# Two-layer attention trunk on one core: q/k copies by DMA, P normalised on ScalarE, and half of the gate projections moved beside branch A's heads

## Chip, core and metric

One core of a Trainium2 chip runs the whole program in one launch. The metric is device time in microseconds (us), from the first to the last instruction of the core. The kernel before was timed three times: 1426.5 us is the median (1426.38 to 1427.1).

## What is computed

A decoder trunk of two layers on 512 tokens of width 1024, all in float32. The reference, cut to one layer:

```python
hdn = rms_norm(x, norm_w)
qa, ka, va, za, qb, kb, vb, zb, ga, gb = split_cols(hdn @ w_in)      # ten blocks of 1024 columns
ya = dilated_mixture(rope(qa), rope(ka), va) * silu(za)              # branch A: 16 heads of 64
ob = diff_attention(rope(qb), rope(kb), vb, lam)                     # branch B: softmax(1) - lam * softmax(2)
yb = rms_norm(ob, subln_w) * (1 - lam_init) * silu(zb)               # 8 heads of 128
merged = sigmoid(ga) * (ya @ w_proj_a) + sigmoid(gb) * (yb @ w_proj_b)
x = x + merged @ w_out
```

After the second layer comes a last RMS norm.

## The kernel before

Every float32 operand of a product is split in two float32r parts, high and low, and each product is three matmuls: high by high, high by low, low by high (lines 282 to 284). A weight block of 128x1024 is loaded by SyncE (line 96), its high part is made on ScalarE (`whi`, line 102) and its low part on VectorE (`wlo`, line 103). A projection (`proj_T`) is a chunk of two such blocks: 48 matmuls of 512 columns, which give two PSUM tiles `pj` (b = 0 and b = 1). Three such PSUM tiles exist; an eviction function turns each into what it is for.

The work of a layer stands in this order: two z chunks and the two v products; then part a, with branch A's heads 0 to 7; part b, with branch B's heads 0 to 6; part c, with B's last head; then the four `pb` chunks and the four output chunks. In parts a to c a main list of chunks is given by the table `parts()`, and the attention steps of the heads are spread evenly among the chunks (`merge`). A scheduler then orders each engine's instructions, and each engine works in that order.

The steps of this study touch the following places. A `qk` chunk gives q (b = 0) and k (b = 1) for a unit: two heads of A, or one of B. Its eviction `ev_qk` (line 398) shuffles the tile on VectorE (`sw`, line 401), multiplies by the rotary tables (line 403 on VectorE, line 404 on GpSimd) and adds (line 405). Then it writes, in 64-partition pieces, the high and low parts of q to `qx` and of k to two tiles `kx`: six ScalarE and six VectorE instructions for a unit (lines 410 to 413, and 419 to 422 twice). The scores need high and low stacked on partitions, so the halves are crossed over.

The attention step of A for one half (one head) makes four blocks of scores (lines 480 to 487), exponentials (line 488, ScalarE, which also sums the denominators), and then `norm` multiplies the four blocks of P by the reciprocal denominators on VectorE (line 531). P is transposed by TensorE (line 506), evicted as high and low (`pt`, lines 507 and 508) and multiplied by v (`o`, line 538). B's `comb` scales both P's (lines 579 to 583).

A `gate` chunk evicts both gates of one row block m (line 693), takes the sigmoid (line 695), and on GpSimd multiplies the A gate by A's projection, which `pa` had written to DRAM and which is loaded back (lines 677 to 697). `pb` adds B's part (lines 704 and 705). In part a stand eight qk and three z chunks, in part b seven qk, the four pa, three z and gates 0 and 1, in part c gates 2 to 7.

Of the kernel before, what the change touches and what calls it, by code (L numbers as in the profile page):

```python
# [23 lines left out]
BIG = 1e30  # L24
SWAP = [(i ^ 8) if i < 16 else i for i in range(32)]
# [7 lines left out]
def trunk_kernel(ctx: ExitStack, tc: tile.TileContext, x, ws, norm_w, subln_w, final_w, lams, negb, rope, ident_in,  # L33
# [15 lines left out]
    x1_dram = dram.tile([DEPTH - 1, NB, P, T], F32, name="x1_dram")  # L49
    v_dram = dram.tile([DEPTH, 2, 8, P, 4, P], F32, name="v_dram")  # L50
# [217 lines left out]
    def proj_T(what, rhs, evac, first=False):  # L268
# [5 lines left out]
        def step(b, k):  # L274
            if b == 0 and k == 0:
                prep_to(j0 + 2)
            if k == 0:
                pool, tag = (pss, "s") if first else (psj, "pj")
                hold[b] = pool.tile([P, T], F32, tag=tag, name=f"pj{c}_{b}")
            ps, hb, o = hold[b], rhs(k), 256 * (k % 4) + b * P  # L280
            w_h, w_l = whi[j0 + k // 4][:, o:o + P], wlo[j0 + k // 4][:, o:o + P]
            nc.tensor.matmul(ps, w_h, hb[:, 0], start=(k == 0), stop=False)  # L282
            nc.tensor.matmul(ps, w_h, hb[:, 1], start=False, stop=False)  # L283
            nc.tensor.matmul(ps, w_l, hb[:, 0], start=False, stop=(k == 7))  # L284
            if b == 1 and k == 3:
                prep_to(j0 + 3)
            if k == 7 and first and b == 1:
                rstd_cols()
                layer_tables()
                for bb in range(2):  # L290
                    evac(bb, hold.pop(bb))
            if k == 7 and not first:
                evac(b, hold.pop(b))
# [103 lines left out]

    def ev_qk(key):
        def f(b, ps):
# [6 lines left out]
            lo, hi = slice(0, 64), slice(64, 128)  # L406
# [114 lines left out]
    def a_pair(layer, u):  # L521
# [48 lines left out]
    def b_head(layer, u):  # L570
# [4 lines left out]
        def comb():  # L575
            r = [small.tile([P, 4], F32, tag=f"rb{h}", name=f"rb{key}{h}") for h in range(2)]
            for h in range(2):
                nc.vector.reciprocal(r[h], store["den", h])
            nc.vector.tensor_scalar(r[1], r[1], nlam[:, layer:layer + 1], None, OP.mult)
            for i in range(4):  # L580
                p, p2 = store["p", 0][i], store["p", 1][i]
                nc.vector.tensor_scalar(p, p, r[0][:, i:i + 1], None, OP.mult)
                nc.vector.scalar_tensor_tensor(p, p2, r[1][:, i:i + 1], p, OP.mult, OP.add)

        def pv(half):
# [16 lines left out]
            for n in range(2):  # L602
                i = 2 * half + n
                scr = small.tile([P, P], F32, tag="sqs", name=f"sqs{key}{i}", bufs=2)
                nc.scalar.activation(scr, o[:, n], AF.Square, accum_out=store["ss"][:, i:i + 1])
            if half == 1:
                r = store["ss"]
                inv_sqrt(r, r, 1.0 / P, 1e-5)
                for i in range(4):
                    nc.vector.tensor_scalar(store["o"][:, i], store["o"][:, i], r[:, i:i + 1], None, OP.mult)  # L610
# [88 lines left out]
    def pb(layer, i):

# [9 lines left out]
        return lambda: proj_T((layer, "pb", i), lambda k: st_["y"][layer, 1, k], ev)  # L710
# [283 lines left out]
```

## Time and profile before

| what | us |
|---|---|
| median of three timed runs | 1426.5 |
| the profiled execution's own time | 1429.07 |
| its span, first to last instruction | 1427.3 |
| TensorE busy | 1376.5 (96%) |
| VectorE busy | 1102.9 (77%) |
| ScalarE busy | 879.0 (62%) |
| GpSimd busy | 166.5 (12%) |

The profile was taken on one execution. A matmul's row begins when it starts, and its end is modelled; since matmuls are pipelined, a row of TensorE overlaps the next one, and a gap between two starts can be partly covered by the row before it. Branch A's heads lie at about 130 to 380 us in the first layer and 830 to 1080 us in the second; branch B's follow, up to about 620 and 1320 us.

### The profile page before, as it was taken

To read this page: it belongs to the slowest core of one execution; us is meant where nothing else is said; L and a number is where in the kernel's file an instruction comes from. 1 tells how busy PE (TensorE), PEld (TensorE's weight loads), DVE (VectorE), ACT (ScalarE), POOL (GpSimd) and SP (SyncE) were. 2 spreads that over 40 slices of the span, in tenths; PEclk is the share of its full clock that TensorE was granted. 3 is DMA by queue.
4 is the path that set the end of the run, shared out by engine and by line. 5 is a ranking of instruction groups with operands and counts; after the bars stand their busy time and mean duration, and the time that the engine had idled before them with its cause. 6 is when DMAs were issued, how large, how long until landed. Compare 5 with 4: busy or idle time off the path is not lost.

```text
span 1427.3 us, 19038 instructions
## 1 busy us (share of the span) xinstructions
PE 1376.5 (96%) x6728; PEld 1144.1 (80%) x6728; DVE 1102.9 (77%) x2252; ACT 879.0 (62%) x1630; POOL 166.5 (12%) x139
## 2 busy tenths in 40 slices
PE   7999999999999999999999999999999999999998
PEld 5788777878788888888878887777878888888898
DVE  6876999999967898645466879999998688975554
ACT  8665667667665668632566666667766567774333
POOL 4100110110101120110220011010110011111000
PEclk9999999999999999999999999999999999999999
DMA  9643222212233323333585242212223322243421
GB/s 300 166 118 118 78 86 65 75 54 82 70 118 101 95 91 110 110 108 103 182 266 132 60 133 82 63 64 82 68 73 96 123 92 85 86 125 94 165 90 66
DMA packets 64607, 152.57 MB, mean 107 GB/s; under 512 B 6016, under 2 KB 22528, under 8 KB 64512
## 3 DMA queue, kind: packets, MB, share of 16 engines
q1 hardware_dynamic: 45312, 134.57, 29.4%
q0 software_dynamic: 2304, 8.39, 3.3%
q10 hardware_dynamic: 16896, 8.39, 2.0%
q8 instruction: 53, 0.87, 0.2%
q14 instruction: 42, 0.34, 0.1%
HBM read 134.55 MB, written 16.78 MB: 106 GB/s over the span
## 4 chain that ended last, share of the span: by engine, by line
PE 67%; DVE 19%; issue 7%; ACT 5%; DMA 1%; POOL 1%; SPq 0%; POOLq 0%; DVEq 0%; ACTq 0%
PE pj L282 16%; PE pj L283 16%; PE pj L284 16%; DVE wlo L103 3%; DVE pt L508 2%; PE X L303 1%; PE X L304 1%; PE X L302 1%; PE pv L302 1%; PE pv L304 1%; PE pv L303 1%; ACT whi L102 1%; DMA T<-ws_d 1%; PE Y L303 1%; POOL sq L206 1%
## 5 line engine op out<-in xcount | busy, mean ns | idle before, releaser
L282 PE MATMUL pj<-h,whi 128*128 128x512 f32 x1024 | 410.1, 402 | 15.0 <-DVE whi L801 6.5
L283 PE MATMUL pj<-h,whi 128*128 128x512 f32 x1024 | 408.0, 398 | 1.2 <-DVE h L189 1.1
L284 PE MATMUL pj<-h,wlo 128*128 128x512 f32 x1024 | 405.6, 398 | 0.0
L102 ACT ACTIVATE whi<-raw 128x1024 fp32r<-128x1024 f32 x207 | 218.7, 1057 | 173.2 <-PE pj L283 114.2
L103 DVE TENSOR_TENSOR wlo<-raw,whi 128x1024 fp32r<-128x1024 f32 x207 | 258.5, 1249 | 83.0 <-ACT whi L102 82.7
L282 PEld LDWEIGHTS pj<-h,whi 128*128 128x128 f32 x1024 | 195.5, 191 | 59.5 <-issue 6.4
L284 PEld LDWEIGHTS pj<-h,wlo 128*128 128x128 f32 x1024 | 195.3, 191 | 39.2 <-DVE wlo L103 0.3
L283 PEld LDWEIGHTS pj<-h,whi 128*128 128x128 f32 x1024 | 195.3, 191 | 39.1 <-DVE h L189 2.9
L103 DVE TENSOR_TENSOR wlo<-T,whi 128x1024 fp32r<-128x1024 f32 x24 | 31.2, 1300 | 14.9 <-ACT whi L102 14.8
L696 POOL TENSOR_TENSOR g<-g,pr 128x512 f32<-128x512 f32 x16 | 21.2, 1326 | 148.0 <-ACT g L695 148.0
L303 PE MATMUL pv<-wlo,mg 128*128 128x256 f32 x128 | 35.7, 283 | 0.0
L304 PE MATMUL pv<-whi,mg 128*128 128x256 f32 x128 | 35.7, 283 | 0.0
L302 PE MATMUL pv<-whi,mg 128*128 128x256 f32 x128 | 35.4, 283 | 0.0
L704 DVE TENSOR_TENSOR g<-pj,g 128x512 f32<-128x512 f32 x16 | 11.1, 692 | 30.5 <-PE pj L284 30.5
L102 ACT ACTIVATE whi<-T 128x1024 fp32r<-128x1024 f32 x24 | 25.1, 1055 | 8.6 <-PE pj L283 2.9
L206 POOL TENSOR_TENSOR sq<-sq,sq 128x512 f32<-128x512 f32 x12 | 19.7, 1638 | 88.6 <-issue 53.4
L708 ACT ACTIVATE mg<-g 128x512 fp32r<-128x512 f32 x16 | 10.1, 632 | 29.5 <-DVE g L705 29.5
L488 ACT ACT_TABLE_LOAD x21 | 26.9, 1283 | 0.3
L302 PE MATMUL X<-whi,h 128*128 128x512 f32 x64 | 24.1, 402 | 2.5 <-DVE z(0, 0, 0)_292 L453 2.5
L693 DVE TENSOR_TENSOR g<-pj,rb 128x512 f32<-128x512 f32 x32 | 22.0, 686 | 5.7 <-PE pj L284 5.6
L303 PE MATMUL X<-wlo,S 128*128 128x512 f32 x64 | 25.1, 393 | 0.8 <-DVE wlo L103 0.8
L303 PE MATMUL Y<-wlo,S 128*128 128x512 f32 x64 | 25.0, 391 | 0.8 <-DVE wlo L103 0.8
(4176 smaller groups left out, 3279.9 us busy)
## 6 DMA issues: line engine op xcount, KB each, us to landing
raw<-ws_d SPq DMA_DIRECT2D x199, 512.0 KB, 3.7
T<-ws_d POOLq DMA_DIRECT2D x16, 512.0 KB, 7.5
v_dram<-c ACTq DMA_DIRECT2D x24, 256.0 KB, 2.6
pa_dram<-pa SPq DMA_DIRECT2D x16, 256.0 KB, 3.1
pr<-pa_dram SPq DMA_DIRECT2D x16, 256.0 KB, 4.0
v_dram<-v ACTq DMA_DIRECT2D x8, 256.0 KB, 5.9
xr<-x_d SPq DMA_DIRECT2D x8, 256.0 KB, 4.4
x_dram<-xr SPq DMA_DIRECT2D x8, 256.0 KB, 3.2
```

The costliest lines, as they stand in the source:

```text
L102: nc.scalar.activation(whi[j], src, AF.Copy)
L103: nc.vector.tensor_tensor(wlo[j], src, bits(whi[j]), OP.subtract)
L206: nc.gpsimd.tensor_tensor(st_["acc"], st_["acc"], s, OP.add)
L282: nc.tensor.matmul(ps, w_h, hb[:, 0], start=(k == 0), stop=False)
L283: nc.tensor.matmul(ps, w_h, hb[:, 1], start=False, stop=False)
L284: nc.tensor.matmul(ps, w_l, hb[:, 0], start=False, stop=(k == 7))
L302: nc.tensor.matmul(ps, hh, w_h, start=first, stop=False, skip_group_check=True)
L303: nc.tensor.matmul(ps, hh, w_l, start=False, stop=False, skip_group_check=True)
L304: nc.tensor.matmul(ps, hl, w_h, start=False, stop=last, skip_group_check=True)
L488: nc.scalar.activation(p, p, AF.Exp, bias=mn[:, i:i + 1], scale=-1.0, accum_out=den[:, i:i + 1])
L508: nc.vector.tensor_tensor(dst[:, 1], ps[:, :n], bits(dst[:, 0]), OP.subtract)
L693: nc.vector.tensor_tensor(g[:, b], ps, rb, OP.mult)
```

## The change

The change has five parts. (1) `ev_qk` makes a high and a low part of the whole 128-partition tile into a new tile `hl` (one ScalarE and one VectorE instruction), and ten DMAs on GpSimd's queue, each of 64 partitions, move the pieces into `qx` and `kx`. (2) A's P is normalised on ScalarE; B's `comb` normalises P relative to the first denominator alone, and the rest goes into the later scale. (3) Gates 0 to 3 of eight stand in part a; their sigmoids are written to DRAM (`g_dram`) by GpSimd's queue. (4) `pa` multiplies by the early gate at its eviction on VectorE, and stores through GpSimd's queue where SyncE's had done it; `pb` loads the early gates and products back through SyncE's queue. (5) The scale of B's output is one instruction where it was four, and the first chunk's eviction in a layer is given a high priority.

```diff
+EARLY = 4
+    g_dram = dram.tile([DEPTH, EARLY, P, 2, T], F32, name="g_dram")
...
+    def move(to, of):
+        nc.gpsimd.dma_start(bits(to), bits(of))
+
     def ev_qk(key):
...
+            hl = b4(f"hl{key}{b}")
+            f_ = -SCALE if b == 0 else 1.0
+            nc.scalar.activation(hl[:, 1], r, AF.Copy, scale=f_)
+            nc.vector.scalar_tensor_tensor(hl[:, 0], r, f_, bits(hl[:, 1]), OP.mult, OP.subtract)
             if b == 0:
                 qx = b4(f"qx{key}")
-                nc.scalar.activation(qx[lo, 0], r[lo], AF.Copy, scale=-SCALE)
-                nc.scalar.activation(qx[hi, 1], r[hi], AF.Copy, scale=-SCALE)
-                nc.vector.scalar_tensor_tensor(qx[hi, 0], r[lo], -SCALE, bits(qx[lo, 0]), OP.mult, OP.subtract)
-                nc.vector.scalar_tensor_tensor(qx[lo, 1], r[hi], -SCALE, bits(qx[hi, 1]), OP.mult, OP.subtract)
+                for half in range(2):
+                    mine = slice(64 * half, 64 * half + 64)
+                    move(qx[0:64, half], hl[mine, 1])
+                    move(qx[64:128, half], hl[mine, 0])
             else:
-                for half, (mine, other) in enumerate(((lo, hi), (hi, lo))):
+                for half in range(2):
                     kx = b4(f"kx{key}{half}")
-                    nc.scalar.activation(kx[mine, 1], r[mine], AF.Copy)
-                    nc.vector.tensor_tensor(kx[mine, 0], r[mine], bits(kx[mine, 1]), OP.subtract)
-                    nc.scalar.activation(kx[other, 0], bits(kx[mine, 1]), AF.Copy)
-                    nc.vector.tensor_copy(kx[other, 1], bits(kx[mine, 0]))
+                    mine = slice(64 * half, 64 * half + 64)
+                    move(kx[0:64], hl[mine])
+                    move(kx[64:128, 0], hl[mine, 1])
+                    move(kx[64:128, 1], hl[mine, 0])
...
-                nc.vector.tensor_scalar(p, p, r[:, i:i + 1], None, OP.mult)
+                nc.scalar.activation(p, p, AF.Copy, scale=r[:, i:i + 1])
...
         def ev(b, ps):
-            t = t2(f"pa{layer}{i}{b}")
-            nc.scalar.activation(t, ps, AF.Copy)
-            nc.sync.dma_start(pa_dram[layer, 2 * i + b], t)
+            if b in g:
+                t = g[b]
+                nc.vector.tensor_tensor(t, ps, t, OP.mult)
+            else:
+                t = t2(f"pa{layer}{i}{b}")
+                nc.scalar.activation(t, ps, AF.Copy)
+            nc.gpsimd.dma_start(pa_dram[layer, 2 * i + b], t)
...
     a = [("qk", 0, u) for u in range(1, 8)] + [("qk", 1, 0)]
-    for s, at in ((2, 4), (3, 7), (4, 10)):
-        a.insert(at, ("z", s // 4, s % 4))
+    for n, at in ((("gate", 0), 1), (("gate", 1), 3), (("z", 0, 2), 6), (("gate", 2), 7), (("z", 0, 3), 10),
+                  (("gate", 3), 11), (("z", 1, 0), 14)):
+        a.insert(at, n)
...
-    c = [("gate", m) for m in range(2, 8)]
+    c = [("gate", m) for m in range(4, 8)]
```

What this does to the engines' orders is shown at three places, all in part a of the first layer.

GpSimd, units 6 and 7 of branch A and unit 0 of branch B in the kernel before (`sw` is the shuffled tile of a unit, q with a 0 behind the bracket and k with a 1; `st` the sine table):

```order
L404 TENSOR_TENSOR sw(0, 0, 6)0_2198<-sw(0, 0, 6)0_2198,st 128x512
L404 TENSOR_TENSOR sw(0, 0, 6)1_2291<-sw(0, 0, 6)1_2291,st 128x512
L404 TENSOR_TENSOR sw(0, 0, 7)0_2542<-sw(0, 0, 7)0_2542,st 128x512
L404 TENSOR_TENSOR sw(0, 0, 7)1_2628<-sw(0, 0, 7)1_2628,st 128x512
L404 TENSOR_TENSOR sw(0, 1, 0)0_2717<-sw(0, 1, 0)0_2717,st 128x512
L404 TENSOR_TENSOR sw(0, 1, 0)1_2805<-sw(0, 1, 0)1_2805,st 128x512
```

GpSimd in the changed kernel, unit 7 and the first row of the next unit:

```order
L410 TENSOR_TENSOR sw(0, 0, 7)0_2898<-sw(0, 0, 7)0_2898,st 128x512
L402 DMA qx(0, 0, 7)_2907<-hl(0, 0, 7)0_2904 64x512 x4
L410 TENSOR_TENSOR sw(0, 0, 7)1_2986<-sw(0, 0, 7)1_2986,st 128x512
L402 DMA kx(0, 0, 7)0_2995<-hl(0, 0, 7)1_2992 64x512
L402 DMA kx(0, 0, 7)0_2995<-hl(0, 0, 7)1_2992 64x1024
L402 DMA kx(0, 0, 7)0_2995<-hl(0, 0, 7)1_2992 64x512
L402 DMA kx(0, 0, 7)1_2999<-hl(0, 0, 7)1_2992 64x1024
L402 DMA kx(0, 0, 7)1_2999<-hl(0, 0, 7)1_2992 64x512 x2
L410 TENSOR_TENSOR sw(0, 1, 0)0_3058<-sw(0, 1, 0)0_3058,st 128x512
```

Each multiplication of the next half or unit now stands behind the moves of the one before, four for q and six for k.

VectorE, the end of the scores of unit 3's first half in the kernel before (`r` is the reciprocal of the denominators, `wlo` a weight's low part):

```order
L487 ISA p(0, 0, 3)0_1768,mn(0, 0, 3)0_1765<-s(0, 0, 3)03_1840,nbt 128x512
L487 ISA mn(0, 0, 3)0_1765 128x1
L528 RECIPROCAL r(0, 0, 3)0_1845<-den(0, 0, 3)0_1766 128x4
L531 TENSOR_SCALAR p(0, 0, 3)0_1768<-p(0, 0, 3)0_1768,r(0, 0, 3)0_1845 128x128
L531 TENSOR_SCALAR p(0, 0, 3)01_1813<-p(0, 0, 3)01_1813,r(0, 0, 3)0_1845 128x256
L531 TENSOR_SCALAR p(0, 0, 3)0_1768<-p(0, 0, 3)0_1768,r(0, 0, 3)0_1845 128x384
L531 TENSOR_SCALAR p(0, 0, 3)0_1768<-p(0, 0, 3)0_1768,r(0, 0, 3)0_1845 128x512
L103 TENSOR_TENSOR wlo_2130<-raw_1907,whi_2129 128x1024
```

VectorE at the same place in the changed kernel (`pt` is an evicted transpose of unit 2):

```order
L497 ISA p(0, 0, 3)0_1874,mn(0, 0, 3)0_1871<-s(0, 0, 3)03_1950,nbt 128x512
L497 ISA mn(0, 0, 3)0_1871 128x1
L538 RECIPROCAL r(0, 0, 3)0_1955<-den(0, 0, 3)0_1872 128x4
L518 TENSOR_TENSOR pt_105<-t((0, 0, 2), 1)2_2068,pt_105 128x256
L105 TENSOR_TENSOR wlo_2077<-raw_1825,whi_2076 128x1024
```

The four multiplications are gone from VectorE; they stand on ScalarE, behind the exponentials.

TensorE, the first scores of unit 7 in the changed kernel (`pj18` and `pj19` are the two chunks that follow unit 7's own, `pj17`; `s` are scores, `h` the normalised input):

```order
L286 MATMUL pj18_1_3078<-h0_7_178,wlo61_2937 128x512
L284 MATMUL pj19_0_3166<-h0_0_129,whi62_3003 128x512
L285 MATMUL pj19_0_3166<-h0_0_129,whi62_3003 128x512
L286 MATMUL pj19_0_3166<-h0_0_129,wlo62_3004 128x512
L284 MATMUL pj19_0_3166<-h0_1_134,whi62_3003 128x512
L285 MATMUL pj19_0_3166<-h0_1_134,whi62_3003 128x512
L490 MATMUL s(0, 0, 7)00_3033<-kx(0, 0, 7)0_2995,qx(0, 0, 7)_2907 128x256
L495 MATMUL s(0, 0, 7)01_3072<-kx(0, 0, 7)0_2995,qx(0, 0, 7)_2907 128x256
```

Between the last matmul of unit 7's k and its first score stand 69 matmuls here, 55 of them of 512 columns; in the kernel before 178 stood there. In the changed kernel units 1, 2, 3, 5 and 7 of A have 69 to 83 such matmuls, in both layers; units 4 and 6 have 120 and 126, and the units of B 101 or more. Of A's units in the kernel before only unit 1 had so few (82).

## Rows read from the trace of the kernel before

**Rows 1.** The profile page: the span.
```profile
span 1427.3 us, 19038 instructions
```

**Rows 2.** Busy time by stretch: us, busy (instructions) of five engines, clock, DMA share, GB/s.
```profile
100.00:400.00 300.00, 285.20 (x1358) 232.53 (x1358) 270.23 (x591) 200.55 (x387) 28.25 (x22) 0.98 0.26 78
400.00:600.00 200.00, 199.04 (x1005) 167.45 (x1004) 156.85 (x367) 131.94 (x275) 23.83 (x20) 1.00 0.33 104
800.00:1100.00 300.00, 286.13 (x1365) 234.27 (x1364) 271.68 (x593) 201.86 (x387) 28.66 (x22) 0.98 0.26 80
...
600.00:700.00 100.00, 100.00 (x455) 83.09 (x454) 50.90 (x65) 36.46 (x53) 10.03 (x7) 1.00 0.38 119
```

**Rows 3.** What TensorE waited for, 100 to 400 us: total, times, longest.
```profile
PE o(0, 0, 0)1_1468 L538 <- DVE pt L508: 2.3, 1, 2.3
PE pj L282 <- DVE rot(0, 0, 4)1_1778 L403: 1.2, 1, 1.2
```

**Rows 4.** Timeline of TensorE: start us, length, instruction, idle before it.
```profile
195.76 0.27 PE L506 MATMUL t((0, 0, 1), 1)1_1658<-ident,p(0, 0, 1)1_1385 128*128 128x128 f32 x1
195.87 0.27 PE L506 MATMUL t((0, 0, 1), 1)1_1658<-ident,p(0, 0, 1)11_1404 128*128 128x128 f32 x1
...
197.96 0.39 PE L486 MATMUL s(0, 0, 2)03_1575<-kx(0, 0, 2)0_1418,qx(0, 0, 2)_1321 128*128 128x512 f32 x1
198.18 0.40 PE L538 MATMUL o(0, 0, 1)1_1731<-pt,vt(0, 0, 1)_1357 128*128 128x512 f32 x1
198.74 0.51 PE L282 MATMUL pj<-h,whi 128*128 128x512 f32 x1 [0.16 <-DVE rot(0, 0, 4)0_1682 L403]
199.08 0.40 PE L283 MATMUL pj<-h,whi 128*128 128x512 f32 x1
199.32 0.40 PE L284 MATMUL pj<-h,wlo 128*128 128x512 f32 x1
```

**Rows 5.** 137 to 317 us: all engines, then TensorE of lines 282, 485 and 506.
```profile
137.00:317.00 180.00, 169.33 (x824) 138.30 (x823) 166.27 (x382) 119.67 (x240) 19.33 (x15) 0.98 0.22 69
...
137.00:317.00 180.00, 68.08 (x167) 32.03 (x166) 0.98 0.22 69
...
137.00:317.00 180.00, 14.90 (x41) 7.72 (x41) 0.98 0.22 69
...
137.00:317.00 180.00, 22.40 (x129) 16.26 (x130) 0.98 0.22 69
```

**Rows 6.** VectorE of lines 531, 412, 413, 420 and 422, in this order.
```profile
100.00:400.00 300.00, 21.34 (x64) 0.98 0.26 78
...
100.00:400.00 300.00, 7.53 (x11) 0.98 0.26 78
...
100.00:400.00 300.00, 8.24 (x11) 0.98 0.26 78
...
100.00:400.00 300.00, 17.23 (x24) 0.98 0.26 78
...
100.00:400.00 300.00, 11.47 (x24) 0.98 0.26 78
```

**Rows 7.** Groups by line: busy, mean ns. Scale from a register, ScalarE and VectorE.
```profile
L429 ACT ACTIVATE c<-c,rstd 128x512 f32<-128x512 f32 x24 | 15.9, 711 | 0.7 <-DVE c L352 0.6
...
L189 DVE SCALAR_TENSOR_TENSOR h<-xr,nw,h 128x512 fp32r<-128x512 f32 x8 | 6.0, 746 | 1.6 <-ACT h L188 1.6
```

**Rows 8.** DMAs on GpSimd's queue (line 112), and the stores of v.
```profile
L112 POOL DMA_DIRECT2D T<-ws_d x16: 861/881/1224, 24.8 to 792.5; - x16
...
DMA to landing us min/median/max: 5.3/7.5/13.1
...
v_dram<-c ACTq DMA_DIRECT2D x24, 256.0 KB, 2.6
```

**Rows 9.** Timeline of GpSimd and VectorE at one time.
```profile
198.25 1.28 POOL L404 TENSOR_TENSOR sw(0, 0, 4)0_1680<-sw(0, 0, 4)0_1680,st 128x512 f32<-128x512 f32 x1 [13.93 <-DVE sw(0, 0, 4)0_1680 L401]
...
198.72 1.09 DVE L422 CAST kx(0, 0, 3)0_1595<-kx(0, 0, 3)0_1595 64x512 fp32r<-64x512 f32 x1
```

More of the change, by code (lines that the diff above doesn't have):

```diff
@@ L287, in step @@
             if k == 7 and first and b == 1:
[L288 to L291, printed above, removed]
+                with tc.high_priority():
+                    rstd_cols()
+                    layer_tables()
+                    for bb in range(2):
+                        evac(bb, hold.pop(bb))
             if k == 7 and not first:
@@ L575, in comb @@
         def comb():
[L576 to L579, printed above, removed]
+            r = small.tile([P, 4], F32, tag="rb0", name=f"rb{key}")
+            q = small.tile([P, 4], F32, tag="rb1", name=f"rq{key}")
+            nc.vector.reciprocal(q, store["den", 1])
+            nc.vector.reciprocal(r, store["den", 0])
+            nc.vector.scalar_tensor_tensor(q, q, nlam[:, layer:layer + 1], store["den", 0], OP.mult, OP.mult)
+            store["r"] = r
             for i in range(4):
                 p, p2 = store["p", 0][i], store["p", 1][i]
-                nc.vector.tensor_scalar(p, p, r[0][:, i:i + 1], None, OP.mult)
-                nc.vector.scalar_tensor_tensor(p, p2, r[1][:, i:i + 1], p, OP.mult, OP.add)
+                nc.vector.scalar_tensor_tensor(p, p2, q[:, i:i + 1], p, OP.mult, OP.add)
         def pv(half):
@@ L603, in pv, with rms, scale @@
                 i = 2 * half + n
+                r = store["r"][:, i:i + 1]
                 scr = small.tile([P, P], F32, tag="sqs", name=f"sqs{key}{i}", bufs=2)
[L605 to L610, printed above, removed]
+                nc.scalar.activation(scr, o[:, n], AF.Square, scale=r, accum_out=store["ss"][:, i:i + 1])
+        def rms():
+            r = store["ss"]
+            inv_sqrt(r, r, 1.0 / P, 1e-5)
+        def scale():
+            r = store["ss"]
+            nc.vector.tensor_tensor(r, r, store["r"], OP.mult)
+            o = store["o"]
+            nc.vector.tensor_tensor(o, o, r.unsqueeze(2).to_broadcast([P, 4, P]), OP.mult)
         def turn():
@@ L633, in values @@
                 return t_steps((key, 0), store, 0) + [(900, lambda: pv(0)), (900, lambda: pv(1))]
-            return [(430, turn)]
+            return [(0, rms), (0, scale), (430, turn)]
         return scores, values
@@ L675, in pa, with pre @@
     def pa(layer, i):
-        def ev(b, ps):
-            t = t2(f"pa{layer}{i}{b}")
-            nc.scalar.activation(t, ps, AF.Copy)
-            nc.sync.dma_start(pa_dram[layer, 2 * i + b], t)
-        return lambda: proj_T((layer, "pa", i), lambda k: st_["y"][layer, 0, k], ev)
+        g = {}
+        def pre():
+            for b in range(2):
+                if 2 * i + b < EARLY:
+                    g[b] = t2(f"ga{layer}{i}{b}")
+                    nc.sync.dma_start(g[b], g_dram[layer, 2 * i + b, :, 0])
+        def ev(b, ps):
+            if b in g:
[5 more added lines that the diff above has]
+            nc.gpsimd.dma_start(pa_dram[layer, 2 * i + b], t)
+        return lambda: [(0, pre)] + proj_T((layer, "pa", i), lambda k: st_["y"][layer, 0, k], ev)
     def gate(layer, m):
         def pre():
-            st_["pa", m] = t2(f"pr{layer}{m}")
-            nc.sync.dma_start(st_["pa", m], pa_dram[layer, m])
+            if m >= EARLY:
+                st_["pa", m] = t2(f"pr{layer}{m}")
+                nc.sync.dma_start(st_["pa", m], pa_dram[layer, m])
         def ev(b, ps):
             if b == 0:
-                st_["g", m] = blk.tile([P, 2, T], F32, tag="b4", name=f"g{layer}{m}")
+                st_["g", m] = f4(f"g{layer}{m}")
             g = st_["g", m]
@@ L695, in ev, with pre @@
                 nc.scalar.activation(g, g, AF.Sigmoid)
-                nc.gpsimd.tensor_tensor(g[:, 0], g[:, 0], st_.pop(("pa", m)), OP.mult)
+                if m < EARLY:
+                    nc.gpsimd.dma_start(g_dram[layer, m], st_.pop(("g", m)))
+                else:
+                    nc.gpsimd.tensor_tensor(g[:, 0], g[:, 0], st_.pop(("pa", m)), OP.mult)
         return lambda: [(0, pre)] + proj_T((layer, "gate", m), hrhs, ev)
     def pb(layer, i):
+        def pre():
+            for m in range(2 * i, 2 * i + 2):
+                if m < EARLY:
+                    g = st_["g", m] = f4(f"gb{layer}{m}")
+                    nc.sync.dma_start(g[:, 1], g_dram[layer, m, :, 1])
+                    nc.sync.dma_start(g[:, 0], pa_dram[layer, m])
         def ev(b, ps):
@@ L709, in ev @@
             nc.vector.tensor_tensor(mm[:, 1], g[:, 0], bits(mm[:, 0]), OP.subtract)
-        return lambda: proj_T((layer, "pb", i), lambda k: st_["y"][layer, 1, k], ev)
+        return lambda: [(0, pre)] + proj_T((layer, "pb", i), lambda k: st_["y"][layer, 1, k], ev)
     def outp(layer, i):
```

5 lines of the change are left out of this document (2 added, 3 removed).

## The prediction

> **What bounds the kernel now.** I read the views from the coarse to the fine: busy time by stretch, then what TensorE waited for, then its timeline, then VectorE's groups. Over the span of 1427.3 us [rows 1] TensorE has little idle time, so the question is where that little lies. The stretches answer it [rows 2]. Beside branch B's heads TensorE is busy 199.04 of 200 us, at full clock, with VectorE busy 156.85 (78%). Where only gates run it is busy 100.00 of 100. Beside branch A's heads it is busy 285.20 of 300 us in the first layer and 286.13 in the second, the mean granted clock is 0.98, and VectorE is busy 270 and 272 of 300 (90%). So A's two stretches are where time is to be had, and VectorE is the engine that is full there. The waits agree: the longest ones end with VectorE, with an eviction of P's transposes or with the rotary product that frees a `pj` tile [rows 3].
>
> The idle time understates the loss, in two ways. The first is the clock: a mean of 0.98 is 0.02 x 300 = 6.0 us of full-speed work a layer. The second is the modelled end of a matmul. Matmuls of 512 columns start 0.22 to 0.24 us apart, yet each row is 0.39 to 0.40 long; the wait at 198.74 came 0.56 after the start before it, so 0.33 was lost and the row shows 0.16 [rows 4]. I therefore priced 180 us of A's stretch by matmul starts [rows 5]. Lines 282 to 284 are one group of three: 3 x 167 at 0.23 us give 115.2. Lines 485 and 486 are 2 x 41 of 384 columns on average, at 0.23 x 384/512 = 0.17: 13.9. The 129 transposes at 0.11 [rows 4] give 14.2. The other 112 (values, first scores; 256 to 512 columns) at 0.16 give 17.9. The sum is 161.2, so 18.8 us are lost: 180 - 169.33 = 10.7 shown as idle, 3.6 by the clock, 4.5 hidden, or 7.5 hidden in 300 us. A pitch of 0.22 instead of 0.23 would add about 5 to the 4.5.
>
> **What the change takes away.** VectorE, in one of A's stretches [rows 6]: normalising P, 21.3 us (64 instructions); writing q and k, 7.5 + 8.2 + 17.2 + 11.5 = 44.5. For the latter come two instructions a unit, 22 for the eleven units in that stretch, at 0.75 [rows 7]: 16.5. Net it loses 49.3 of 270.2, which leaves 221. Four gates come in: 4 x 48 matmuls at 0.23 are 44 us of TensorE, and where gates ran alone VectorE was busy 51% [rows 2], so at most 22 us of VectorE. A's stretch becomes some 320 us with 243 of VectorE: 76%, the level of B's stretch, 78%. That is my reason to expect B's loss rate there.
>
> The gain if A's stretches run as B's do: idle falls from 14.8 and 13.9 to 0.96 x 300/200 = 1.4 each, 13.4 + 12.4 = 25.8; the clock gives 2 x 6.0 = 12.0; of the hidden 7.5 I count 6 a layer, 12. Together 49.8 us, from a bound below of 25.8 (the shown idle alone).
>
> ScalarE takes the 64 normalisations at no more than 0.71 each [rows 7], 45 us, gives up four of six 64-partition copies a unit, and gets 16 us with the gates (36% of 44, rows 2 show the share). It is at 200.55 of 300; even 262 of 320 is 82%, so it is not the bound, and I put it at nothing. If its queue is not free when a normalisation is due, the transposes behind it wait; that is in the first rival.
>
> **What the change adds.** Ten moves a unit on GpSimd. The trace has no such move. The nearest rows are the accumulating DMAs of the same queue, twice as many partitions: 0.88 us of GpSimd (1.22 at most), landing after 5.3 to 13.1 us, median 7.5; and the plain stores of v from another queue, 2.6 us [rows 8]. A unit then costs GpSimd 10 x 0.88 + 2 x 1.28 [rows 9] = 11.4 us, against at least 22 us that a pair of chunks takes, so the queue keeps up. What counts is latency, at the places where the order leaves least room. For unit 7 there are 69 matmuls between its k and its first score: 55 x 0.23 + 10 x 0.11 + 4 x 0.15 = 14.3 us. The chain is shuffle, add and low part on VectorE (at most 0.75 each), the GpSimd product 1.28, the high part 0.71, three moves 2.6: 6.9 us. Seven other VectorE instructions stand between, at most 5.3, of which 2.0 lie beside GpSimd and ScalarE: 10.2. Then the landing. At 2.6 the score would be 1.5 us early, at 7.5 it waits 3.4. I take a third of 3.4, 1.1 us, since a move is nearer to the stores (no accumulation, a quarter to half of the bytes). Five units a layer have 69 to 83 matmuls, so ten places: 11 us, between 0 and 34. Unit 3 has all ten moves queued behind its second product, and seven of them precede its first score; it is the one most sensitive to the price of a move.
>
> The Trainium skill, DMA: Bandwidth & Descriptors, section "Anatomy of one DMA", gives such a DMA about 2.0 us and bytes/436 GB/s: 2.3 us for 128 KB, an estimate. By that the charge would be nothing and the sum -50; rows 8 show 7.5 us, for an accumulation of four times the bytes.
>
> The rest: GpSimd gets A's stores and loses eight gate products of 1.3 us (as the rows of its products, rows 9); SyncE's queue loses 16 stores and gets 16 net loads of early gates and products. A load for `pb` that came late would hold its eviction and then a `pj` tile; up to 3 us a layer, taken as nothing, because `pb` stands where TensorE has slack in PSUM tiles. The moves load the DMA engines: 32 units x 1.5 MB, in A's stretch 12 MB beside 78 GB/s x 300 us = 23 MB at a share of 0.26 [rows 2]: about 0.4, not a bound. In B's stretches 1 us can be won in all [rows 2], so I count nothing.
>
> **Sum.** -49.8 + 11 = -39 on the profiled execution's 1429.07 (its span is 1427.3): 1390. The median of the timed runs is 2.6 below that execution, so 1388.
>
> **Rivals.**
> *Half of it.* VectorE is freed, but A's chain (scores, exponential on ScalarE, reciprocal on VectorE, normalisation on ScalarE, transposes) gets one more crossing between engines, and in-order queues wait in its place. For: all queues are in order, and in A both halves are transposed, in B one. Against: VectorE is no longer full. 1403 to 1420, say 1411.
> *Slower: moves land late.* The place is the ten tight scores. Ten waits of 5 us eat the gain; by the chain above that is a landing of 14.3 + 5 - 10.2 = 9.1 us, which lies inside 5.3 to 13.1 [rows 8]. At 10.5 us each wait is 6.4: 64 - 50 = +14, 1440; at 13.1 it is 1466. Against: those rows accumulate from DRAM.
> *Slower: descriptors starve.* GpSimd and VectorE do disturb each other: a cast of 64x512 that overlaps the GpSimd product took 1.09 us [rows 9], where the mean is 11.47/24 = 0.48 [rows 6]. If a move took 2.2 us, unit 3's seven would take 9 us more; with some 5 us at each tight place, the gain is gone: 1427 to 1450. Against: the casts and the normalisations are what the change removes from VectorE, and the accumulating DMAs never took over 1.22. The skill's SBUF — State Buffer, "Who interferes with whom", says that a copy, cast or tensor-scalar on VectorE locks GpSimd's descriptors out; it gives 0.62 us alone and 3.1 beside a copy. The casts in rows 9 agree that there is a lock, and no move is shown.
> *No effect.* The waits are latency of A's chain, not VectorE's load; then idle only moves: 1424 to 1429.
>
> **How the numbers follow.** Forecast 55%: 1376 to 1410, likeliest 1388. Half 20%. Slower 17% (late landing 12, starved 5). No effect 6%. More than 50 us: 2%. A time within 0.2% (2.9 us) cannot be told from no change. Faster 0.77, same 0.06, slower 0.17. The range reaches over the second case and to the edge of no effect, 1370 to 1425; about 18% lies above it and 2% below.
>
> **What would show it.** Right: TensorE busy over 98% of A's stretch and the clock at 0.99 or 1.00; VectorE near 75% there; GpSimd's moves near 0.9 us, landing under 5; first scores of units 2, 3, 5, 7 with waits under 2 us. Wrong: waits of TensorE for a DMA into `kx` or `qx` over 5 us; VectorE still at 90%; or ScalarE as the releaser of transposes.

## The result

The changed kernel takes 1414.26 us (median of four runs, 1410.13 to 1414.5) beside 1426.8 for the kernel before on the same chip: a ratio of 0.990, 95% interval 0.988 to 0.992. It is 12.5 us faster; 39 were forecast. The profiled execution took 1414.27.

The page of the profile after: the span, busy time by engine, and the row of GpSimd's DMA queue (packets, MB, share).

```profile
span 1412.5 us, 19604 instructions
...
PE 1364.1 (97%) x6728; PEld 1140.0 (81%) x6728; DVE 983.4 (70%) x1908; ACT 862.2 (61%) x1630; POOL 339.0 (24%) x475
...
q0 software_dynamic: 22144, 67.13, 19.9%
```

The span is 14.8 us shorter than [rows 1]. The stretches that answer to [rows 2], after the change (us, busy of TensorE, its weight loads, VectorE, ScalarE, GpSimd, clock, DMA share, GB/s):

```profile
100.00:400.00 300.00, 298.25 (x1462) 248.10 (x1461) 229.16 (x465) 211.60 (x405) 83.11 (x130) 1.00 0.55 149
400.00:600.00 200.00, 191.84 (x955) 160.79 (x954) 140.24 (x321) 115.41 (x260) 53.24 (x75) 0.98 0.48 135
...
800.00:1100.00 300.00, 297.27 (x1465) 247.45 (x1464) 223.77 (x475) 209.82 (x414) 84.89 (x129) 1.00 0.57 155
...
1200.00:1300.00 100.00, 91.92 (x457) 76.68 (x456) 69.89 (x156) 58.38 (x125) 22.70 (x30) 0.97 0.41 115
```

Branch A's stretches did what was forecast: 298.25 and 297.27 busy of 300, clock 1.00, VectorE at 76 and 75%. Branch B's stretch did not stay as it was: 191.84 of 200, where [rows 2] have 199.04. TensorE's longest waits after the change, in all, times and longest, say where:

```profile
PE pj L284 <- DVE whi L842: 6.0, 1, 6.0
PE ot(0, 1, 4)_4994 L633 <- DVE of(0, 1, 4)_4856 L628: 5.6, 1, 5.6
PE ot(1, 1, 4)_11228 L633 <- DVE of(1, 1, 4)_11090 L628: 5.6, 1, 5.6
PE pj L284 <- DVE gb L745: 2.1, 1, 2.1
PE pj L284 <- ACT yb(1, 1, 7)_12029 L639: 1.5, 1, 1.5
PE s(1, 0, 7)00_9267 L490 <- DMA kx(1, 0, 7)0_9229<-hl(1, 0, 7)1_9226: 1.5, 1, 1.5
```

The first is the program's start and was 6.5 before. The next two are new: `ot` is the transposition of a finished head's output, head 4 of branch B in each layer. TensorE's timeline there (start us, length, instruction, idle before it) shows that the order has almost nothing between the head's last values (`o`) and `ot`:

```profile
531.29 0.75 PE L605 MATMUL o(0, 1, 4)1_4890<-vt(0, 1, 4)_4627,pt 128*128 128x256 f32 x5
531.88 0.40 PE L496 MATMUL s(0, 1, 5)13_5010<-kx(0, 1, 5)1_4750,qx(0, 1, 5)_4664 128*128 128x512 f32 x1
532.11 0.39 PE L284 MATMUL pj<-h,whi 128*128 128x512 f32 x1
532.34 0.39 PE L285 MATMUL pj<-h,whi 128*128 128x512 f32 x1
532.57 0.39 PE L286 MATMUL pj<-h,wlo 128*128 128x512 f32 x1
538.51 1.11 PE L633 MATMUL ot(0, 1, 4)_4994<-ident,of(0, 1, 4)_4856 128*128 128x128 f32 x4 [5.56 <-DVE of(0, 1, 4)_4856 L628]
```

Meanwhile the head's normalisation crosses engines: the squares on ScalarE wait behind a weight's high part and an exponential, then come the root on GpSimd (line 242) and the scale on VectorE, behind four instructions of the next head (line 595). The timelines of ScalarE, GpSimd and VectorE:

```profile
532.82 1.06 ACT L104 ACTIVATE whi<-raw 128x1024 fp32r<-128x1024 f32 x1 [0.35 <-PE pj L285]
533.78 0.71 ACT L498 ACTIVATE p(0, 1, 5)1_4934<-p(0, 1, 5)1_4934,mn(0, 1, 5)1_4931 128x512 f32<-128x512 f32 x1
...
534.88 0.39 ACT L618 ACTIVATE sqs(0, 1, 4)3_4909<-of(0, 1, 4)_4856,rb(0, 1, 4)_4725 128x128 f32<-128x128 f32 x1
...
535.64 1.04 POOL L242 TENSOR_TENSOR rs(0, 1, 4)_4857<-rs(0, 1, 4)_4857,mhalf 128x4 f32<-128x4 f32 x1 [5.48 <-DVE rs(0, 1, 4)_4857 L241]
...
536.38 1.28 DVE L595 SCALAR_TENSOR_TENSOR p(0, 1, 5)0_4788<-p(0, 1, 5)1_4934,rq(0, 1, 5)_5016,p(0, 1, 5)0_4788 128x384 f32<-128x384 f32 x2
537.57 0.16 DVE L626 TENSOR_TENSOR rs(0, 1, 4)_4857<-rs(0, 1, 4)_4857,rb(0, 1, 4)_4725 128x4 f32<-128x4 f32 x1
537.76 0.69 DVE L628 TENSOR_TENSOR of(0, 1, 4)_4856<-of(0, 1, 4)_4856,rs(0, 1, 4)_4857 128x512 f32<-128x512 f32 x1
```

From the end of `o` (532.04) to the start of `ot` it takes 6.5 us, covered by less than 1 us of matmuls: four stand between them. In the kernel before 42 stood there, 9.1 us by their pitches, and the other heads have 6.1 us or more in the changed one. The clock follows (TensorE busy, clock, DMA share, GB/s):

```profile
530.00:537.00 7.00, 2.95 (x20) 1.00 0.55 146
537.00:543.80 6.80, 5.25 (x18) 0.50 0.26 99
543.80:550.00 6.20, 6.20 (x32) 1.00 0.26 53
```

TensorE had been idle since 532.96; from 537.0 on the granted clock is 0.50 (1.2 of 2.4 GHz) for 6.8 us. One such place thus costs 5.6 of idle time and some 3.4 by the clock.

The second loss is behind the last matmul. Rows of the program's end before, then after: SyncE's last waits, GpSimd's final DRAIN, and SyncE's own short drain, which marks the end of its waits for DMAs (durations min/median/max ns, first and last start; the starts behind GpSimd's long drain are the program's last steps).

```profile
L989 SPq EVENT_SEMAPHORE  x11: 17/28/28, 1424.5 to 1427.2; - x11
L989 POOLq DRAIN  x3: 40/102/1979, 1422.5 to 1427.0; - x3
L989 SPq DRAIN  x3: 7/7/7, 1426.4 to 1426.7; - x3
```
```profile
L1031 SPq EVENT_SEMAPHORE  x11: 17/28/28, 1403.4 to 1412.4; - x11
L1031 POOLq DRAIN  x3: 46/93/10302, 1401.4 to 1412.2; - x3
L1031 SPq DRAIN  x3: 7/7/7, 1405.3 to 1412.0; - x3
```

GpSimd's drain took 1.98 us before and ended 1.98 us ahead of SyncE's; after the change it takes 10.30 and ends 6.34 us behind SyncE's, at 1411.72. No other engine works then.

**The account.** I add up, over consecutive starts of matmuls, what exceeds the pitch of the first one's shape (0.227 us for 512 columns, 0.175 for 384, 0.120 for 256, 0.060 for 128), where the excess is over 5 ns. "A" is 100 to 400 and 800 to 1100 us, "B" 400 to 650 and 1100 to 1350; "end" is the span behind the drain that closes SyncE's waits (1405.4 us in the changed kernel).

| kernel | median us | lost in A | lost in B | elsewhere | end | GpSimd's DMAs, drain us |
|---|---|---|---|---|---|---|
| before | 1426.8 | 79.2 | 20.1 | 17.4 | 0.8 | 16, 1.98 |
| changed | 1414.3 | 33.6 | 46.2 | 16.0 | 7.1 | 360, 10.30 |
| gates alone | 1433.7 | 48.8 | 55.8 | 17.5 | 0.8 | 40, 3.93 |
| B's normalisation alone | 1427.8 | 80.2 | 17.3 | 16.8 | 0.8 | 16, 1.98 |
| moves alone | 1397.3 | 45.4 | 20.1 | 14.9 | 5.2 | 336, 8.34 |
| P on ScalarE alone | 1417.2 | 66.9 | 21.0 | 17.5 | 0.8 | 16, 1.97 |
| changed, all gates back | 1390.8 | 44.9 | 14.7 | 15.1 | 6.5 | 352, 9.65 |
| changed, two gates early | 1379.8 | 30.8 | 17.9 | 15.3 | 6.8 | 356, 9.98 |
| changed, gates 4, 5 into B | 1410.5 | 30.9 | 48.5 | 14.0 | 7.1 | 360, 10.30 |
| two early, root by sqrt | 1374.6 | 31.3 | 17.8 | 15.6 | 0.8 | 356, 10.44 |

From before to changed: -45.6 in A, +26.1 in B, -1.4 elsewhere, +6.3 at the end, together -14.6 of the span's -14.8. The 0.060 is too low: transposes, the matmuls of 128 columns, start 0.108 us apart (median, in both kernels). So 9 to 12 us of each number under A, and 6 to 8 under B, are no loss but the transposes' own time; with 0.108 the steps are -45.5 in A and +25.6 in B.

### The profile page after: what moved, and what is told of

It reads as the page before. It is cut to its first block, busy times and chain, and to the rows that moved or that the text cites. A ratio compares the mean times of both kernels' runs of the same rounds, so it can differ in the third digit from the quotient of the medians.

```text
span 1412.5 us, 19604 instructions
## 1 busy us (share of the span) xinstructions
PE 1364.1 (97%) x6728; PEld 1140.0 (81%) x6728; DVE 983.4 (70%) x1908; ACT 862.2 (61%) x1630; POOL 339.0 (24%) x475
## 3 DMA queue, kind: packets, MB, share of 16 engines
q0 software_dynamic: 22144, 67.13, 19.9%
## 4 chain that ended last, share of the span: by engine, by line
PE 76%; ACT 7%; DVE 7%; issue 4%; DMA 3%; POOL 2%; SPq 0%; POOLq 0%; ACTq 0%; DVEq 0%
PE pj L284 17%; PE pj L285 17%; PE pj L286 17%; PE X L306 2%; PE X L307 2%; PE X L305 2%; ACT whi L104 1%; PE Y L306 1%; PE Y L307 1%; PE Y L305 1%; DVE wlo L105 1%; PE pv L305 1%; PE pv L307 1%; PE pv L306 1%; DMA raw<-ws_d 1%
## 5 line engine op out<-in xcount | busy, mean ns | idle before, releaser
L105 DVE TENSOR_TENSOR wlo<-raw,whi 128x1024 fp32r<-128x1024 f32 x207 | 273.5, 1322 | 98.9 <-ACT whi L104 96.1
L728 POOL DMA_DIRECT2D g_dram<-g x8 | 4.5, 564 | 132.1 <-ACT g L726 132.1
L730 POOL TENSOR_TENSOR g<-g,pr 128x512 f32<-128x512 f32 x8 | 10.6, 1322 | 82.3 <-ACT g L726 49.2
L114 POOL DMA_DIRECT2D T<-ws_d x16 | 14.7, 935 | 50.1 <-ACT T L113 42.3
L306 PE MATMUL X<-wlo,h 128*128 128x512 f32 x64 | 25.1, 391 | 0.4 <-DVE wlo L105 0.4
L307 PE MATMUL Y<-whi,S 128*128 128x512 f32 x64 | 24.9, 389 | 0.0
```

Of the source, the lines that this page charges most:

```text
L105: nc.vector.tensor_tensor(wlo[j], src, bits(whi[j]), OP.subtract)
L114: nc.gpsimd.dma_start(out=flat(t), in_=add, accum_op=OP.add)
L306: nc.tensor.matmul(ps, hh, w_l, start=False, stop=False, skip_group_check=True)
L307: nc.tensor.matmul(ps, hl, w_h, start=False, stop=last, skip_group_check=True)
```

## The experiments

All ratios are to the kernel before on the same chip, with their 95% interval.

**One part at a time.** Four kernels are the kernel before with one part of the change each. Gates alone (the new table, `g_dram`, `pa` gated at its eviction):

> The kernel before with the fourth part of the change alone: gates 0 to 3 beside A's heads and kept in DRAM, A's projection gated at its eviction; q and k, P and branch B's normalisation as before, 40 software DMAs on GpSimd where there were 16. Theory 1 (the gates cost B's stretches what covered the turn of a head's output): with gates 0 and 1 gone from there, TensorE's order has 1.4 to 3.8 us of other work between a head's last values and the transposes of its output for heads 0, 2 and 4, 5.8 us or more before; so the waits of those transposes come back here, 2 to 4 us each, with TensorE at 94 to 98% of 500 to 600 us. A's stretches win a part only (VectorE 270 + 22 of some 344 us, 85%), 10 to 25 us in both layers. Time 1410 to 1430. Theory 2 (branch B's new chain of scale is the cause): B's stretches stay at 99%, no transposes of the output wait over 1 us, and the time is lower by all that A wins, 1402 to 1415.

Measured 1433.68, 1.0044 (1.0029 to 1.0059): slower. The waits of `ot` came back without any other part of the change:

```profile
PE ot(0, 1, 4)_4948 L620 <- DVE of(0, 1, 4)_4839 L615: 3.9, 1, 3.9
PE ot(1, 1, 4)_11166 L620 <- DVE of(1, 1, 4)_11057 L615: 3.9, 1, 3.9
PE ot(0, 1, 2)_4374 L620 <- DVE of(0, 1, 2)_4263 L615: 3.4, 1, 3.4
PE ot(1, 1, 2)_10592 L620 <- DVE of(1, 1, 2)_10481 L615: 3.4, 1, 3.4
```

A wins 30 us by them, B loses 36. Head 0, with 3.8 us between, does not wait; the time is 3.7 above my range, the mechanism is theory 1's. Branch B's new normalisation alone:

```diff
-                nc.vector.tensor_scalar(p, p, r[0][:, i:i + 1], None, OP.mult)
-                nc.vector.scalar_tensor_tensor(p, p2, r[1][:, i:i + 1], p, OP.mult, OP.add)
+                nc.vector.scalar_tensor_tensor(p, p2, q[:, i:i + 1], p, OP.mult, OP.add)
...
-            return [(430, turn)]
+            return [(0, rms), (0, scale), (430, turn)]
```

> The kernel before with branch B's new normalisation alone: P's halves combined in one pass, squares with a scale, the root and the scaling as steps of their own. Theory 1 (the gates): the order keeps 7.1 us or more of other work ahead of the transposes of each output, so no such wait over 1 us, B's stretches stay at 99%, time 1424 to 1428. Theory 2 (the chain itself, 6.5 us from the end of the values to the transposes in the changed kernel, with steps on four engines): waits of 2 to 6 us for several of the 16 heads, 10 to 30 us in all, 1436 to 1456.

Measured 1427.8, 1.0004 (0.9994 to 1.0013): no difference, B's stretches up to 600 and 1300 us 99.59 busy of 100 or more, no wait of `ot`. The chain alone does not bring the wait. The moves alone, and P on ScalarE alone:

```diff
+    def move(to, of):
+        nc.gpsimd.dma_start(bits(to), bits(of))
```

> The kernel before with the copies of q and k by DMA alone, 320 moves on GpSimd in place of 64-partition copies. VectorE loses 28 us in each of A's stretches, from 90% to some 81%. Theory 1: A's stretches win something near half of the 44 us that the changed kernel wins there, 15 to 25, B's stretches stay at 99%, and the end loses some 8 us, since GpSimd's last drain grows with its number of DMAs (1.98 us with 16 of them, 10.30 with 360: 24 ns each): 1410 to 1420, the last drain 9 to 10.5 us. Rival: the drain does not go by the number of DMAs: it stays at 2 us and the time is 1402 to 1412. Rival: the moves are late in B's stretches: waits of first scores for a move of 1 us or more there.

Measured 1397.34, 0.979 (0.9775 to 0.9804): 30 us faster, more than twice the whole change and 13 below my range. The drain is 8.34 (my range 9 to 10.5), the loss at the end 4.4. No first score in B waited for a move.

```diff
-                nc.vector.tensor_scalar(p, p, r[:, i:i + 1], None, OP.mult)
+                nc.scalar.activation(p, p, AF.Copy, scale=r[:, i:i + 1])
```

> The kernel before with A's P normalised on ScalarE alone. VectorE loses 21 us in each of A's stretches. Theory: the long waits of A's values for the eviction of transposes and the waits for pj tiles get shorter, 8 to 18 us in both layers; B's stretches and the end as before: 1409 to 1419. Rival (one more crossing between engines in A's chain): transposes of A's P wait for ScalarE's normalisation, and the time is not under 1425.

Measured 1417.16, 0.993 (0.9915 to 0.9944): 10.6 us faster than that chip's 1427.77, as expected. The first rows here are of the kernel with the moves alone, the second of the one with P on ScalarE alone, 100 to 400 us, columns as above:

```profile
100.00:400.00 300.00, 295.16 (x1456) 246.45 (x1455) 252.85 (x569) 181.89 (x363) 89.93 (x135) 0.99 0.54 146
```
```profile
100.00:400.00 300.00, 287.78 (x1393) 237.62 (x1392) 252.01 (x534) 228.71 (x457) 28.45 (x23) 0.99 0.26 80
```

VectorE is equally busy in both (253 and 252 of 300, 84%), yet TensorE is idle 4.8 us in one and 12.2 in the other. So VectorE's share is not the whole cause of A's loss, which my sum had made it. The two differ in which instructions went (those between a unit's rotary product and its scores, or those between scores and transposes) and in ScalarE, 182 and 229; no run here tells these apart.

The four parts add up to -35 us (+5.9, 0, -30.4, -10.6), the whole change gives -12.5. By the account the parts win 76 us in A when each is taken alone, and the whole 46: they win the same idle time more than once, while what B and the end lose is lost in full. The fifth part's high priority was not run by itself.

**The gates put back.** The changed kernel with the old table of parts:

```diff
-EARLY = 4
+EARLY = 0
...
-    c = [("gate", m) for m in range(4, 8)]
+    c = [("gate", m) for m in range(2, 8)]
```

> The changed kernel with the gates back where they were: all eight after the heads as before (two of them among branch B's last chunks), nothing kept in DRAM but A's projection; the moves, P on ScalarE and branch B's new scale chain stay. Theory (moving the gates cost more than all else won): alone, the moves of q and k gave -30 and P on ScalarE -11, both at A's idle time of some 40 us a layer, so together -33 to -41; branch B's stretches stay over 98% with no wait of an output's transposes over 1 us: 1386 to 1394, the last drain of GpSimd 8.3 to 9.7 us. Rival (the early gates are needed to dilute A's work on VectorE): A's stretches stay at 97% or less, 1400 or more.

Measured 1390.82, 0.9745 (0.973 to 0.9759), 23 us faster than the change as a whole. B loses 14.7 there, in place of 46.2.

**Two gates early.** Gates 0 and 1 stand among A's heads, gates 2 and 3 where the kernel before had 0 and 1:

```diff
-EARLY = 4
+EARLY = 2
...
-    for n, at in ((("gate", 0), 1), (("gate", 1), 3), (("z", 0, 2), 6), (("gate", 2), 7), (("z", 0, 3), 10),
-                  (("gate", 3), 11), (("z", 1, 0), 14)):
+    for n, at in ((("gate", 0), 2), (("z", 0, 2), 5), (("gate", 1), 7), (("z", 0, 3), 9), (("z", 1, 0), 12)):
...
+                  (("gate", 2), 11), (("z", 1, 3), 14), (("gate", 3), 15)):
```

> The changed kernel with two gates beside A's heads in place of four; gates 2 and 3 go among branch B's last chunks, where before had gates 0 and 1, gates 4 to 7 behind as in the changed kernel. Theory (what branch B's stretches lost is the two chunks of gates that stood there): the transposes of an output have 8.3 us or more of other work ahead of them, B's stretches are back at 98% or more, and some 17 to 25 us are won against the changed kernel: 1389 to 1398, the drain 8.5 to 10. Rival (keeping gates in DRAM costs by itself, at the loads for A's and B's projection): 1400 or more, with B's stretches still under 96% or waits for a loaded gate over 3 us.

Measured 1379.84, 0.9667 (0.9653 to 0.9681): 34 us faster than the changed kernel, 9 better than I expected. A and B are both full:

```profile
100.00:400.00 300.00, 298.71 (x1480) 250.57 (x1479) 233.99 (x490) 210.84 (x421) 92.34 (x142) 1.00 0.56 152
400.00:600.00 200.00, 200.00 (x1009) 168.53 (x1008) 138.91 (x308) 125.60 (x256) 48.27 (x65) 1.00 0.45 134
```

So two early gates fill A as four do (30.8 and 33.6 lost), B loses 17.9 in place of 46.2, and keeping gates in DRAM costs little: the longest wait put down to it is 1.3 us, a first score behind a gate's store.

**Number of chunks, or the place?** Four early gates, and gates 4 and 5 among B's last chunks, so that B has as many chunks as before:

```diff
-                  (("z", 1, 3), 13)):
+                  (("gate", 4), 11), (("z", 1, 3), 14), (("gate", 5), 15)):
...
-    c = [("gate", m) for m in range(4, 8)]
+    c = [("gate", m) for m in range(6, 8)]
```

> The changed kernel, four gates beside A's heads as it has them, with gates 4 and 5 put among branch B's last chunks, so that B's heads have 16 chunks beside them as before the change; only gates 6 and 7 stay behind. The order now leaves 8.7 us or more of other work ahead of the transposes of heads 0 to 5 of branch B, 1.2 us for head 6 and none for head 7. Theory 1 (what costs is a place where nothing stands between a head's values and the transposes of its output, wherever it is): the wait of 5.6 us at head 4 goes, and one of 3 to 6 us each comes at heads 6 and 7, in both layers, with the clock at half after it: 1405 to 1425. Theory 2 (what costs is the number of chunks beside B's heads): TensorE at 98% or more from 400 us to the end of branch B's heads, 1380 to 1392.

Measured 1410.5, 0.9887 (0.9873 to 0.99). The wait moved to where the order now leaves no work, as theory 1 says:

```profile
PE ot(0, 1, 7)_5794 L633 <- DVE of(0, 1, 7)_5733 L628: 4.1, 1, 4.1
PE ot(1, 1, 7)_12028 L633 <- DVE of(1, 1, 7)_11967 L628: 3.8, 1, 3.8
PE ot(1, 1, 6)_11876 L633 <- DVE of(1, 1, 6)_11783 L628: 3.4, 1, 3.4
PE ot(0, 1, 6)_5642 L633 <- DVE of(0, 1, 6)_5549 L628: 3.4, 1, 3.4
```

It is not how much work stands beside B's heads, but whether some stands between `o` and `ot`. Why the scheduler leaves a given place bare was not settled.

**The moves on other queues.** The kernel with all gates back, its moves issued by ScalarE (`nc.scalar.dma_start`) or SyncE (`nc.sync.dma_start`):

> As the kernel with all gates back, and the 320 moves issued from ScalarE's queue in place of GpSimd's. Theory (GpSimd's last drain goes by the DMAs that it issued, 20 ns for each move, and ends last): the drain is 2 to 3.5 us, the span ends within 1 us of SyncE's last wait, and 4.5 to 6 us are won against the kernel with all gates back, unless ScalarE pays for the issues. Rival: each issue holds ScalarE's queue as SyncE's issues hold theirs, 0.33 to 0.43 us (ten a unit: 3.3 to 4.3 us), the exponentials and splits behind it come later, and what the drain gives back is lost in the heads' stretches: 0 to 10 us slower than the kernel with all gates back.

> As the kernel with all gates back, and the 320 moves issued from SyncE's queue in place of GpSimd's. Theory: the drain as in the run with ScalarE's queue, 4.5 to 6 us won against the kernel with all gates back. Rival: a move waits in SyncE's queue behind a load of weights that waits for its buffer; first scores wait 2 us or more for a move, at five or more places, and the time is 5 to 20 us above the kernel with all gates back.

On ScalarE 1439.5, 1.0083 (1.0058 to 1.0108); on SyncE 1406.9, 0.9859 (0.9843 to 0.9876): 49 and 16 us slower than from GpSimd. The drain did shrink, to 3.28 us in both, and the span ends 0.8 us behind SyncE's last wait. But each issue held ScalarE 0.47 to 2.42 us (median 0.61, 207 us in all), first scores waited up to 2.9 us for a move, and A lost 91.5: the rival's mechanism, at 49 us where it had at most 10. From SyncE (median 0.59, 204 us) A lost 64.2. There no first score waited 2 us for a move, which the rival needed; the two longest waits behind the program's start (4.2 and 4.1 us) are of B's scores behind VectorE, which itself waited 4.1 and 4.3 us there for a move of k. The rest of the 16 us is spread over waits for `pj` tiles and was not traced to one cause.

**The drain alone.** The last instruction of GpSimd in the program is the root of the final norm. Taken off GpSimd, by a logarithm and an exponential on ScalarE in the kernel with two early gates:

```diff
-                nc.gpsimd.tensor_tensor(rs[:, 1:2], rs[:, 0:1], mhalf[:, 0:1], OP.pow)
+                nc.scalar.activation(rs[:, 1:2], rs[:, 0:1], AF.Ln)
+                nc.scalar.activation(rs[:, 1:2], rs[:, 1:2], AF.Exp, scale=-0.5)
```

> The kernel with two early gates (1380 us) with one more edit: the four roots of the final norm on ScalarE, as a logarithm and an exponential, in place of GpSimd's power. GpSimd's last instruction is then some 70 us ahead of the end. Theory (the last drain starts behind GpSimd's last instruction, takes about 10 us with 356 DMAs and ends 6.0 us after SyncE's last wait): it runs beside the last projection, the span ends within 1 us of SyncE's last wait; 6 us are won, less 1 to 3 us for ScalarE's tables of functions at the end: 1375 to 1378. Rival (the drain is part of the program's end whatever stands before it): it still ends 6 us after SyncE, 1380 to 1383.

Measured 1381.19, 0.9681 (0.9667 to 0.9694): nothing won. The drain did move (10.44 us from 1278.6 on, the span ends 0.8 us behind SyncE), but ScalarE loaded a table of 1.28 us twice for each of four blocks, and SyncE's last drain came 8.0 us later. The time is the rival's, the mechanism another. So, with a square root and a reciprocal, in that kernel and in the changed one:

```diff
-                nc.gpsimd.tensor_tensor(rs[:, 1:2], rs[:, 0:1], mhalf[:, 0:1], OP.pow)
+                nc.scalar.activation(rs[:, 1:2], rs[:, 0:1], AF.Sqrt)
+                nc.vector.reciprocal(rs[:, 1:2], rs[:, 1:2])
```

> The kernel with two early gates with the four roots of the final norm off GpSimd in a cheaper way: a square root on ScalarE and a reciprocal on VectorE. With the logarithm and the exponential ScalarE loaded two tables of 1.28 us for each of the four column blocks, and the end came 8 us later than it was, which ate the 6 us; with one function alone one load should do. Theory: the last drain again lies beside the last projection, the span ends within 1 us of SyncE's last wait, and that wait is at most 1.5 us later than with GpSimd's power: 1373.5 to 1376. Rival: the table is loaded for each block again, 1.3 us or more each: 1377 to 1381.

> The changed kernel with that edit alone, four early gates and all else as it is. Theory (6.3 of its span are the last drain, which ends that much later than SyncE's last wait): 1407.5 to 1410, with the two waits of 5.6 us in branch B's stretches as they were. Rival: the drain's end is not what the changed kernel lost: 1413 to 1416.

With two early gates 1374.55, 0.9632 (0.9619 to 0.9645), as forecast and the fastest kernel of the study. ScalarE's one table load for the four roots, and the rows of the end:

```profile
1361.05 1.28 ACT L802 ACT_TABLE_LOAD   x1
```
```profile
L1031 SPq EVENT_SEMAPHORE  x12: 17/28/28, 1370.6 to 1373.3; - x12
L1031 POOLq DRAIN  x3: 46/93/10437, 1278.8 to 1373.1; - x3
```

The drain is no shorter (10.44 where it was 9.98), but starts at 1278.8 and lies beside matmuls. In the changed kernel the edit gave 1403.74, 0.9843 (0.983 to 0.9857), 10.5 us below it where 6.3 were expected. The two waits of `ot` stood (5.5 us each); the last matmul began 4.0 us earlier with the same order. Of that, 3 us are smaller losses in A and B by the account above (31.6 and 45.2): a first score waited 1.5 us for a move in the changed kernel alone, and behind the first wait of `ot` the clock is at half for 3.4 us in place of 6.8. The rest is open; the changed kernel's own runs differ by 4.4 us.

## Why the prediction was wrong

**What bounds the kernel, and A's gain: right.** The forecast for A was -49.8 and +11 for late scores, -39; A gave -45.6 in all. The gross term was right, and the late scores were mis-sized. Of ten tight places one waited for a move (1.5 us) where 11 us were charged. Moves cost GpSimd less than the 0.88 us that I took, and landed earlier than 7.5 us. Unit 7's moves of q (min/median/max ns), and the landing of all moves:

```profile
L402 POOL DMA_DIRECT2D qx(0, 0, 7)_2907<-hl(0, 0, 7)0_2904 x4: 518/527/544, 321.6 to 323.4; - x4
...
DMA to landing us min/median/max: 2.2/4.5/8.7
```

The reason given, VectorE's share, was too simple, as the two kernels at 84% show. The load on the DMA engines was taken too low: the working gives the moves 12 MB of A's stretch, but the eleven units that it counts there for VectorE make 16.5, and the share came to 0.55 and 0.57 where some 0.4 was expected. Nor do gates alone run in the stretch of 600 to 700 us, from which VectorE's share beside gates was taken: the values of B's last head stand at 607 to 616. The 76% that came of it was met all the same. All signs named for a right forecast came true, with the moves even cheaper, and still the time was missed: they look at A alone.

**"In B's stretches 1 us can be won in all [rows 2], so I count nothing": the step that failed.** It asked what B could win, not what it could lose. The change took gates 0 and 1 out from among B's last heads. I priced them where they went and not where they came from. B lost 26.1 us; two waits of `ot` with the clock behind them are 2 x 9 = 18 of it. Another 4 stand at the start of `pb` in the second layer (the waits of 1.5 and 2.1 us above: for the last head's output, and for a loaded gate); the rest was not traced. The experiments show this three ways: the gates alone bring it, B's normalisation alone does not, and with two gates left among B's chunks it is gone.

**The end of the program: a term that was missing.** 344 more DMAs on GpSimd lengthen its final drain by 8.3 us, 6.3 beyond SyncE's last wait. The moves were priced as issue and landing only.

**The loads for `pb`, "up to 3 us a layer, taken as nothing".** The one wait for a loaded gate is 2.1 us, in the second layer: within the bound, not nothing.

**The rivals.** "Half of it" gave 1403 to 1420 and holds the time, for a wrong reason: no transposes of A's P waited for ScalarE's normalisation for long. "Moves land late" and "descriptors starve" did not happen: the slowest of the changed kernel's 320 moves took 0.60 us of GpSimd. With the moves alone, where P is still normalised on VectorE, seven took more, each beside such multiplications (`TENSOR_SCALAR`), and the longest 1.23:

```profile
1030.52 1.23 POOL L399 DMA_DIRECT2D kx(1, 1, 2)0_9560<-hl(1, 1, 2)1_9557  x1
```
```profile
1030.76 0.29 DVE L587 TENSOR_SCALAR p(1, 1, 0)0_9339<-p(1, 1, 0)0_9339,rb(1, 1, 0)0_9614 128x128 f32<-128x128 f32 x1
1030.95 0.35 DVE L587 TENSOR_SCALAR p(1, 1, 0)01_9388<-p(1, 1, 0)01_9388,rb(1, 1, 0)0_9614 128x256 f32<-128x256 f32 x1
1031.21 0.81 DVE L587 TENSOR_SCALAR p(1, 1, 0)0_9339<-p(1, 1, 0)0_9339,rb(1, 1, 0)0_9614 128x384 f32<-128x384 f32 x2
```

The 292 moves there with less than 0.1 us of them beside took 0.59 at most. The rival's mechanism is thus seen, small, and the change removes these multiplications, as the prediction held against the rival. The Trainium skill, SBUF — State Buffer, "Who interferes with whom", lets a copy, cast or tensor-scalar on VectorE hold such a move up; the run with the moves alone agrees in kind. The Trainium skill's rule for one DMA (DMA: Bandwidth & Descriptors, "Anatomy of one DMA"), an estimate of 2.3 us for 128 KB, is the minimum here (2.2), half of the median of 4.5: the measurement decides.

## What to carry to other kernels

Work that moves to fill one stretch leaves another: price the place that it comes from, and look in the new order for chains over several engines whose end an in-order engine reaches with nothing put between. When a change adds many small DMAs to GpSimd's queue, look at the end of the program too, and let GpSimd's last instruction stand early enough for its drain to lie beside other work. A busy share tells where to look, but two edits that lower it equally may be worth 10 or 30 us.

## Hardware that I had not expected

GpSimd's drain at the program's end goes by the DMAs that it issued in the whole program. The 320 moves of 64 partitions add 6.37 us (19.9 ns each, from the moves alone), 24 DMAs of 128 partitions from SBUF to DRAM add 1.95 (81 ns each, from the gates alone, 8 of 512 KB and 16 of 256); 1.98 and these two make the 10.30 of the changed kernel. With all gates back, 16 of 256 KB add 1.30, again 81 ns each, so with these it goes by their number and not by their bytes. Why a move costs a quarter of that no run tells: it has half the partitions and another target. The drain starts behind GpSimd's last instruction, whenever that stands: at 1278.8, 94 us ahead of the end, it took 10.44.

A DMA issue of the same move holds GpSimd 0.52 us, SyncE 0.59 and ScalarE 0.61 (medians), with up to 1.83 and 2.42 on the last two, and up to 1.23 on GpSimd beside VectorE's tensor-scalar multiplications, 0.60 without them.
